# Layer-1 MLP: weight-block sums and weight splits moved from VectorE into transfers issued by GpSimd

## The chip, the cores and the metric

The kernel runs on one core of one Trainium2 chip. The metric is the device time of one execution in microseconds (us), as the median of several runs of the same program. Lines are named as in the profile (L887 is line 887 of the kernel before); the changed kernel has ten lines more ahead of most of them, so that its listings show L93, L94, L95 for the new helper and L1218 for what was L1208.

## The reference

The model is a two-layer trunk over 512 latent tokens and 256 context tokens of width 1024. Layer 0 mixes tokens with an mLSTM, layer 1 with windowed attention, and each mixer is followed by a squared-ReLU MLP of hidden width 4096. The change touches only the MLP of layer 1, which sees the latent tokens alone:

```python
def _sq_relu_mlp(u, w1, w2):
    return jnp.square(jax.nn.relu(u @ w1)) @ w2
...
h = h + mod_l[5] * _sq_relu_mlp(_modulate(_rms_norm(h, norm_ffn[i]), mod_l[3], mod_l[4]),
                                ffn_w1[i], ffn_w2[i])
...
return _rms_norm(h, final_norm)
```

All inputs are float32, and the result must keep more accuracy than one pass of TensorE in its reduced float32 type (called fp32r in the profile).

## The kernel before, in words

**Splits.** Every matrix operand is split in two fp32r parts: `hi`, the value cast to fp32r, and `lo`, the value minus `hi`. A product is then three matmuls (`mm3`, L96 to L98): hi by hi, hi by lo, lo by hi. A split (`split`, L884) is one ScalarE copy into `whi` (L887) and one VectorE subtraction into `wlo` (L888).

**Weight units and the ring.** Weights come in units of 128 partitions by 1024 float32 values (512 KB). `unit` (L73) loads a unit into a buffer named `raw` by a transfer issued on SP's queue (L80) and splits it into `whi` and `wlo`. These buffers stand in a ring with 4 `whi`, 4 `wlo` and 3 `raw` buffers. So a unit may be loaded into `raw` before a `whi` buffer comes free, and only the split waits for the buffer.

**The MLP of layer 1** (`ffn1`, with its list of weight units from `plan1`) treats the second matrix product as products of 2 by 2 blocks: tokens in two halves, hidden features in two halves, output columns in two halves. Seven block products instead of eight are enough when sums of blocks are multiplied. The work goes in four steps, `steps1`: three steps of 8 hidden tiles of 128 features and one of 4; the last 4 hidden tiles are done plainly. Each step has two parts:

- the w1 part (`hidden`): for each hidden tile one unit of `w1`, 24 matmuls of 512 columns. In the first step the first four units are taken together, in pieces of 256 columns, the later halves unit by unit.
- the w2 part (`product`): seven products, in the order 1, 2, 3, 5, 6, 7, 4 by number, each with one or two units of `w2`. The blocks of `w2` are called 11, 12, 21, 22 (feature half, output half) and lie in buffers named `wb`. `less` (L1208) forms the differences of blocks in place on VectorE: 12-11 first, then 22-12, 22-11 and 22-21 as the products ask for them. The sums of the hidden blocks are formed on VectorE in `second` (L1313 to L1315), the seven results are put together in `join`.

**The order.** Python code writes the instructions in the order of `plan`: after each unit of work that TensorE has finished, `feed` takes the next entry of the list, so that four units stand ahead of TensorE at any time. A scheduler then gives each engine its own order, which is in-order at run time: an instruction that waits holds up everything behind it on its engine, transfers that the engine issues among them. Before the change GpSimd (POOL) issues no transfer; all weights come by SP's queue.

**Buffers for transfers.** The kernel's last function makes the program with `dynamic_dma_scratch_size=512` (L1997); the change leaves that as it is.

Of the kernel before, what the change touches and what calls it, by code (L numbers as in the profile page):

```python
# [21 lines left out]
P = 128  # L22
D = 1024
KT = D // P
NL = 512
# [31 lines left out]
class Trunk:  # L57
# [15 lines left out]
    def unit(self, src, eng=None):  # L73

        nc = self.nc
        if len(src.shape) == 3:
            src = src.rearrange("m p c -> p m c")
        n = int(np.prod(src.shape[1:]))
        raw = self.ring.tile([P, D], F32, name="raw", tag="raw", bufs=self.nraw)[:, :n]
        nc.sync.dma_start(out=raw if len(src.shape) == 2 else raw.rearrange("p (m c) -> p m c", m=src.shape[1]), in_=src)  # L80
        hi = self.ring.tile([P, D], F32R, name="whi", tag="whi", bufs=self.nsplit)[:, :n]
        lo = self.ring.tile([P, D], F32R, name="wlo", tag="wlo", bufs=self.nsplit)[:, :n]
        self.split(raw, hi, lo, eng)
        if self.ada_cap and self.ada_todo and self.ada_todo[0][:2] < self.ada_cap:
            self.ada_step()
        return hi, lo

    def take(self, eng=None):
# [1101 lines left out]
    def plan1(self):  # L1190

        nc, a = self.nc, self.a
        self.steps1 = [(0, 4), (8, 4), (16, 4), (24, 2)]
        self.w2r = w2r = {}
        at = 0

        def load(b, u, n):
            def f():  # L1200
                t = w2r[b, u] = self.fp.tile([P, D], F32, name=f"wb{b}", tag=f"w{b}{u}")
                nc.sync.dma_start(out=t, in_=a["w2b"][n])
            return f

        def less(o, x, y, u):

            def f():
                nc.vector.tensor_tensor(out=w2r[o, u], in0=w2r[x, u], in1=w2r[y, u], op=ALU.subtract)  # L1208
            return f

        def w1(m, *extra):
            def f():
                r = self.unit(a["w1"][1, m])
                for x in extra:
                    x()
                return r
            return f

        def w2(b, u, *extra):
            def f():  # L1220
                hi, lo = [self.ring.tile([P, D], F32R, name=n, tag=n, bufs=self.nsplit) for n in ("whi", "wlo")]
                self.split(w2r[b, u], hi, lo)
                for x in extra:
                    x()
                return hi, lo
            return f
        self.plan, self.begun = [], []
        for base, nk in self.steps1:
            us = range(nk // 2)
            extra = []  # L1230
            for b in (12, 22, 11, 21):
                extra += [load(b, u, at + (11, 12, 21, 22).index(b) * len(us) + u) for u in us]
            extra += [less(12, 12, 11, u) for u in us]
            at += 4 * len(us)
            ms = [base + nk * i + k for k in range(nk) for i in range(2)]
            skip = 0 if base else 2
            per = -(-len(extra) // (len(ms) - skip))
            self.plan += [w1(m) for m in ms[:skip]]
            self.plan += [w1(m, *extra[per * i:per * i + per]) for i, m in enumerate(ms[skip:])]
            self.plan += [w2(b, u) for b in (11, 21) for u in us]  # L1240
            self.plan += [w2(22, u, less(22, 22, 12, u)) for u in us]
            self.plan += [w2(12, u, less(11, 22, 11, u)) for u in us]
            self.plan += [w2(22, u, less(21, 22, 21, u)) for u in us]
            self.plan += [w2(b, u) for b in (11, 21) for u in us]
# [12 lines left out]
        self.plan += [w1(m) for m in range(self.last1, 4 * KT)]  # L1257
        self.plan += [w2_plain(i) for i in range(4 * KT - self.last1)]

    def ffn1(self, u, out):  # L1260

        nc, tc, a = self.nc, self.tc, self.a
        xs = self.xs(u)
        fp = self.fp
        H = NL // 2
        tt = nc.vector.tensor_tensor
# [40 lines left out]
        def second(m, m0, k):  # L1307

            r0, r1, s34 = rt.pop(m0), rt.pop(m), rt.pop(("34", k))
            hid["12", k] = two("h12", k)  # L1310
            self.split(r1, *hid["12", k])
            s = fp.tile([P, NL], F32, name="s12", tag="s12", bufs=2)
            tt(out=s[:, 0:H], in0=r0[:, H:NL], in1=r1[:, H:NL], op=ALU.add)  # L1313
            tt(out=s[:, H:NL], in0=s[:, 0:H], in1=r0[:, 0:H], op=ALU.subtract)
            tt(out=s34[:, H:NL], in0=r1[:, 0:H], in1=s[:, H:NL], op=ALU.subtract)  # L1315
            for n, src in (("1", s), ("3", s34)):
                hid[n, k] = two("e" + n, k)
                self.split(src, *hid[n, k])
# [67 lines left out]
        def join(i):  # L1386
            a1, a3, a4, a5, a6 = [acc[p, i] for p in (1, 3, 4, 5, 6)]
            x = fp.tile([P, NL], F32, name="r", tag="r", bufs=4)
            for o, l, r, op in ((a6, a1, a6, ALU.add), (a1, kept[2, i], a1, ALU.add), (x, kept[7, i], a6, ALU.add),
                                (a6, a6, a5, ALU.add), (a3, a3, a6, ALU.add), (a4, x, a4, ALU.subtract),  # L1390
                                (a5, x, a5, ALU.add)):
                tt(out=o, in0=l, in1=r, op=op)
            for t, d, o in ((i, 0, a1), (i, 1, a3), (2 + i, 0, a4), (2 + i, 1, a5)):
                tt(out=o, in0=o, in1=self.grow[:, d * 512:(d + 1) * 512], op=ALU.mult)
                y = res[t][:, d * 512:(d + 1) * 512]
                tt(out=y, in0=y, in1=o, op=ALU.add)
        hp = []
        for n, m in enumerate(range(self.last1, 4 * KT)):
            hidden([m], square)
            hp.append(two("h12", n))  # L1400
            self.split(rt.pop(m), *hp[n])
            turn((0, 2, 1, 3)[n])
            if n % 2:
                join(n // 2)
# [600 lines left out]
```

## Time and profile before

| what | value |
|---|---|
| median of 3 runs | 1549.54 us (1549.34 to 1550.19) |
| the profiled execution | 1551.29 us, of which its span is 1549.4 us |
| MLP of layer 1 in the span | about 1208 us to the end |
| TensorE, VectorE, ScalarE, GpSimd busy | 1509.6, 1127.1, 740.2, 326.5 us |
| granted TensorE clock, mean | 0.992 |

The span runs from the first to the last instruction of the profiled execution; what is outside it is 1.9 us. PE is TensorE, DVE is VectorE, ACT is ScalarE, POOL is GpSimd, SP is the engine whose queue issues most transfers. Matmuls overlap each other, so the duration of one (389 ns) is longer than the distance between two starts.

### The profile page before, as it was taken

The numbers are of one execution on the slowest core, as the hardware profiler recorded it, in microseconds if no ns is written. First come the engines' busy times: TensorE is split into PE (matmuls) and PEld (weight loads), VectorE is DVE, ScalarE is ACT, GpSimd is POOL, SyncE is SP. The second block draws the span as 40 slices with busy tenths as digits, with TensorE's granted clock in tenths as the row PEclk, the third lists the DMA queues.
The fourth block names the chain that finished last, engine by engine and source line by source line (L and its number), as shares of the span: only waits on it lengthen the run. The fifth ranks groups of instructions, "written<-read, shape, count | busy, mean of one in ns | idle before, by whom it ended". The sixth has DMA issues, their size and how long they took to land.

```text
span 1549.4 us, 23838 instructions
## 1 busy us (share of the span) xinstructions
PE 1509.6 (97%) x9110; PEld 1355.9 (88%) x9110; DVE 1127.1 (73%) x2084; ACT 740.2 (48%) x1501; POOL 326.5 (21%) x318
## 2 busy tenths in 40 slices
PE   6999999999999999999999999999999999999998
PEld 4778888878889999999999999888887988888886
DVE  3684657488797888767676667778888875757697
ACT  4533343344573332524424355666666665545454
POOL 0322111113203222232224221243443100000000
PEclk8999999999999999999999999999999999999999
DMA  8422323234231343343443422011111424150321
GB/s 316 139 83 69 125 82 118 73 116 150 74 110 42 120 139 124 125 146 125 148 145 100 150 69 66 32 34 42 42 41 43 177 83 149 41 163 28 109 69 55
DMA packets 47848, 157.27 MB, mean 102 GB/s; under 512 B 5327, under 2 KB 8911, under 8 KB 47607
## 3 DMA queue, kind: packets, MB, share of 16 engines
q1 hardware_dynamic: 46560, 154.25, 30.3%
q8 instruction: 72, 1.18, 0.3%
q10 hardware_dynamic: 1175, 1.51, 0.3%
q14 instruction: 41, 0.34, 0.1%
HBM read 153.64 MB, written 2.10 MB: 101 GB/s over the span
## 4 chain that ended last, share of the span: by engine, by line
PE 79%; DVE 6%; issue 4%; ACT 4%; POOL 3%; DMA 1%; POOLq 0%; DVEq 0%; ACTq 0%
PE mm L96 17%; PE mm L97 16%; PE mm L98 16%; PE p L98 2%; PE p L97 2%; PE p L96 2%; PE pt L1825 2%; PE pj L96 1%; PE pj L97 1%; PE pj L98 1%; PE at L843 1%; DVE adap L262 1%; PE av L1840 1%; ACT whi L887 1%; DVE wlo L888 1%
## 5 line engine op out<-in xcount | busy, mean ns | idle before, releaser
L888 DVE TENSOR_TENSOR wlo<-raw,whi 128x1024 fp32r<-128x1024 f32 (+2 forms) x152 | 179.6, 1186 | 82.3 <-ACT whi L887 80.6
L887 ACT CAST whi<-raw 128x1024 fp32r<-128x1024 f32 (+2 forms) x155 | 154.0, 999 | 141.9 <-PE mm L97 77.4
L96 PE MATMUL mm<-uH,whi 128*128 128x512 f32 (+1 forms) x496 | 189.4, 386 | 0.0
L97 PE MATMUL mm<-uL,whi 128*128 128x512 f32 (+1 forms) x496 | 186.7, 378 | 0.7 <-DVE uL L332 0.4
L98 PE MATMUL mm<-uH,wlo 128*128 128x512 f32 (+1 forms) x496 | 186.9, 378 | 0.0
L262 DVE SCALAR_TENSOR_TENSOR adap<-raw,crow 128x1024 bf16<-128x1024 f32 x128 | 165.8, 1295 | 19.9 <-DMA raw<-ada 19.1
L96 PE MATMUL mm<-h,whi 128*128 128x384 f32 x512 | 172.9, 338 | 1.9 <-ACT h L887 1.9
L97 PE MATMUL mm<-h,whi 128*128 128x384 f32 x512 | 172.6, 337 | 0.5 <-DVE h L888 0.5
L98 PE MATMUL mm<-h,wlo 128*128 128x384 f32 x512 | 172.1, 336 | 0.0
L887 ACT CAST whi<-sum 128x512 fp32r<-128x512 f32 (+1 forms) x42 | 31.9, 761 | 165.8 <-PE mm L97 75.9
L98 PEld LDWEIGHTS mm<-uH,wlo 128*128 128x128 f32 x496 | 93.4, 188 | 17.9 <-issue 0.9
L97 PEld LDWEIGHTS mm<-uL,whi 128*128 128x128 f32 x496 | 93.6, 189 | 16.4 <-DVE uL L489 0.7
L96 PEld LDWEIGHTS mm<-uH,whi 128*128 128x128 f32 x496 | 92.9, 189 | 15.6 <-issue 0.3
L96 PEld LDWEIGHTS mm<-h,whi 128*128 128x128 f32 x512 | 96.1, 188 | 2.8 <-ACT h L887 2.8
L97 PEld LDWEIGHTS mm<-h,whi 128*128 128x128 f32 x512 | 96.1, 188 | 1.5 <-DVE h L888 1.4
L98 PEld LDWEIGHTS mm<-h,wlo 128*128 128x128 f32 x512 | 96.1, 188 | 0.0
L888 DVE TENSOR_TENSOR wlo<-wb,whi 128x1024 fp32r<-128x1024 f32 x49 | 59.2, 1221 | 35.9 <-ACT whi L887 35.8
L888 DVE TENSOR_TENSOR h<-r,h 128x384 fp32r<-128x384 f32 (+2 forms) x100 | 56.4, 568 | 34.1 <-ACT h L887 33.8
L887 ACT CAST whi<-wb 128x1024 fp32r<-128x1024 f32 x49 | 51.6, 1054 | 60.9 <-PE mm L97 27.1
L1809 POOL TENSOR_SCALAR e<-e,den 128x512 f32<-128x512 f32 (+1 forms) x64 | 49.0, 779 | 135.1 <-DVE den L1807 86.9
L98 PE MATMUL p<-t,wlo 128*128 128x384 f32 x224 | 75.4, 337 | 0.5 <-DVE wlo L888 0.5
L97 PE MATMUL p<-t,whi 128*128 128x384 f32 x224 | 75.2, 336 | 0.0
(401 smaller groups left out, 4180.0 us busy)
## 6 DMA issues: line engine op xcount, KB each, us to landing
raw<-ada SPq DMA_DIRECT2D x80, 512.0 KB, 3.6
raw<-w SPq DMA_DIRECT2D x64, 512.0 KB, 3.5
raw<-w2a SPq DMA_DIRECT2D x32, 512.0 KB, 3.5
wb<-w2b SPq DMA_DIRECT2D x28, 512.0 KB, 4.2
adaw<-ada SPq DMA_DIRECT2D x16, 512.0 KB, 7.7
hL<-xT SPq DMA_DIRECT2D x16, 256.0 KB, 3.5
raw<-wqk SPq DMA_DIRECT2D x8, 512.0 KB, 4.0
raw<-wv SPq DMA_DIRECT2D x8, 512.0 KB, 3.5
```

The costliest lines, as they stand in the source:

```text
L96: mm(out=out, lhsT=ah, rhs=bh, start=start, stop=False)
L97: mm(out=out, lhsT=ah, rhs=bl, start=False, stop=False)
L98: mm(out=out, lhsT=al, rhs=bh, start=False, stop=stop)
L262: self.tc.keep_in_program_order(nc.vector.scalar_tensor_tensor(out=pr, in0=w, scalar=0.5, in1=self.crow[:, v, :], op0=ALU.mult, op1=ALU.mu ...
L843: mm(out=o[hh][:, i * VW:(i + 1) * VW], lhsT=pw[g, d, hh][:, i, :], rhs=v[:, 3 * g + i, hh, :], start=False, stop=i == 2)
L887: keep(self.nc.scalar.copy(out=hi, in_=src))
L888: keep((eng or self.nc.vector).tensor_tensor(out=lo, in0=src, in1=hi.bitcast(F32), op=ALU.subtract))
L1809: nc.gpsimd.tensor_scalar(out=out[ii][:, :W], in0=out[ii][:, :W], scalar1=den[:, ii:ii + 1], scalar2=1.0, op0=ALU.mult, op1=ALU.mult)
L1825: nc.tensor.transpose(out=pt[:, i * P:(i + 1) * P], in_=ps_[i][:, n * P:(n + 1) * P], identity=self.ident)
L1840: mm(out=o, lhsT=vv, rhs=ph, start=n == 0, stop=False)
```

## The change

- Each unit of `w1` in layer 1 no longer passes through `raw`. `unit_dma` loads it from HBM straight into `whi` with a transfer that casts; ScalarE writes the negative of `whi` into `wlo` (`Copy` with scale -1, L94); a second transfer from HBM adds the unit onto `wlo`. Both transfers are issued by POOL (L93, L95).
- The block differences of `w2` become sums formed by transfers that add onto the block in place, issued by POOL (`more`, L1218): 12 += 11 first, then 22 += 12, and 21 += 22. The buffer of block 11 is loaded a second time, with block 12 by SP's queue, and block 22 is added onto it from HBM.
- The signs of the block products are turned to fit: in `second` and `join` some additions become subtractions and the other way round; two operations of `join` have other operands. Their number and sizes stay.

```diff
+    def unit_dma(self, src):
+        nc = self.nc
+        hi, lo = [self.ring.tile([P, D], F32R, name=n, tag=n, bufs=self.nsplit) for n in ("whi", "wlo")]
+        nc.gpsimd.dma_start(out=hi, in_=src)
+        nc.scalar.activation(out=lo, in_=hi.bitcast(F32), func=AF.Copy, scale=-1.0)
+        nc.gpsimd.dma_start(out=lo, in_=src, accum_op=ALU.add)
         return hi, lo
...
-        def less(o, x, y, u):
+        def more(o, x, u, n=None):
...
-                nc.vector.tensor_tensor(out=w2r[o, u], in0=w2r[x, u], in1=w2r[y, u], op=ALU.subtract)
+                nc.gpsimd.dma_start(out=w2r[o, u], in_=w2r[x, u] if n is None else a["w2b"][n], accum_op=ALU.add)
...
-                r = self.unit(a["w1"][1, m])
+                r = self.unit_dma(a["w1"][1, m])
...
-            for b in (12, 22, 11, 21):
-                extra += [load(b, u, at + (11, 12, 21, 22).index(b) * len(us) + u) for u in us]
-            extra += [less(12, 12, 11, u) for u in us]
+            for b in (11, 12, 21, 22):
+                extra += [load(b, u, block(b, u)) for u in us]
+            extra += [more(12, 11, u) for u in us]
...
-            self.plan += [w2(b, u) for b in (11, 21) for u in us]
-            self.plan += [w2(22, u, less(22, 22, 12, u)) for u in us]
-            self.plan += [w2(12, u, less(11, 22, 11, u)) for u in us]
-            self.plan += [w2(22, u, less(21, 22, 21, u)) for u in us]
+            self.plan += [w2(11, u, load(11, u, block(12, u)), more(11, 22, u, block(22, u))) for u in us]
+            self.plan += [w2(21, u) for u in us]
+            self.plan += [w2(22, u, more(22, 12, u)) for u in us]
+            self.plan += [w2(12, u) for u in us]
+            self.plan += [w2(22, u, more(21, 22, u)) for u in us]
             self.plan += [w2(b, u) for b in (11, 21) for u in us]
```

How the change moves instructions is read from the two programs. First POOL. Before, the last rows of its list are these: the sums of squares of the norm ahead of the MLP (`ssB`), its power (`rc`), and then nothing until the four powers of the final norm.

```order
L295 TENSOR_TENSOR nAuH_12565<-nAuH_12565,nAuL_12566 128x256
L313 TENSOR_TENSOR rc<-rs,mhalf 128x2
L295 TENSOR_TENSOR ssB<-ssB,sq 128x256 x6
L313 TENSOR_TENSOR rc<-rs,mhalf 128x2
L1425 TENSOR_TENSOR ss_15627<-ss_15627,mhalf 128x1 x4
```

In the changed program the same place begins so; `w` in a row is the layer's `w1` in HBM, `wb_13088` and `wb_13090` are the two units of block 12, `wb_13079` and `wb_13081` those of block 11.

```order
L305 TENSOR_TENSOR ssB<-ssB,sq 128x256
L93 DMA whi<-w 128x1024
L305 TENSOR_TENSOR ssB<-ssB,sq 128x256 x3
L93 DMA whi<-w 128x1024
L305 TENSOR_TENSOR ssB<-ssB,sq 128x256
L95 DMA wlo<-w 128x1024
L305 TENSOR_TENSOR ssB<-ssB,sq 128x256
L95 DMA wlo<-w 128x1024
L323 TENSOR_TENSOR rc<-rs,mhalf 128x2
L93 DMA whi<-w 128x1024 x3
L1218 DMA wb_13088<-wb_13079 128x1024
L95 DMA wlo<-w 128x1024 x3
```

Four transfers now stand among the sums and ahead of the power, and behind it the transfers of the first step follow one another, the `lo` of the fifth unit behind three `whi` transfers and one block sum.

Second, POOL at the passage from the first step's w2 part to the second step's w1 part, where before it has no row at all. With the buffers' numbers: `wb12_13782` and `wb12_13784` are block 12 of the second step, `whi_13768` and `wlo_13769` are the first unit of its `w1`.

```order
L1218 DMA wb12_13782<-wb11_13773 128x1024
L1218 DMA wb12_13784<-wb11_13775 128x1024
L93 DMA whi_13768<-w1 128x1024
L93 DMA whi_13777<-w1 128x1024
L95 DMA wlo_13769<-w1 128x1024
L93 DMA whi_13816<-w1 128x1024
L95 DMA wlo_13778<-w1 128x1024
L93 DMA whi_13825<-w1 128x1024
L95 DMA wlo_13817<-w1 128x1024
```

The first unit's cast now stands behind the two sums for block 12, and its `lo` behind the second unit's cast. Over the whole program POOL issues 92 transfers: 32 casts, 32 additions onto `wlo`, 28 additions onto blocks.

Third, VectorE at the same passage, before. The rows are the splits and differences of the last two products of the first step (`wb11`, `wb21`), the first differences of the second step, and the splits of its first units.

```order
L888 TENSOR_TENSOR wlo_13705<-wb11_13282,whi_13704 128x1024
L1208 TENSOR_TENSOR wb12_13778<-wb12_13778,wb11_13828 128x1024
L888 TENSOR_TENSOR wlo_13739<-wb21_13304,whi_13738 128x1024
L1208 TENSOR_TENSOR wb12_13780<-wb12_13780,wb11_13830 128x1024
L888 TENSOR_TENSOR wlo_13743<-wb21_13306,whi_13742 128x1024
L888 TENSOR_TENSOR wlo_13775<-raw_13772,whi_13774 128x1024
L888 TENSOR_TENSOR wlo_13785<-raw_13782,whi_13784 128x1024
L888 TENSOR_TENSOR wlo_13825<-raw_13822,whi_13824 128x1024
```

In the changed program the split of the last block is followed at once by the work on the hidden values:

```order
L898 TENSOR_TENSOR wlo_13739<-wb21_13277,whi_13738 128x1024
L1319 TENSOR_TENSOR s34_13873<-r_13859 128x256
L898 TENSOR_TENSOR h11_13870<-r_13859,h11_13869 128x256
L1327 TENSOR_TENSOR s12_13911<-r_13859,r_13900 128x256
L1328 TENSOR_TENSOR s12_13911<-s12_13911,r_13859 128x256
```

All block differences and all splits of `w1` are gone from VectorE's list there. On SP's queue 32 loads of `raw` are gone, and 7 loads of `w2` (block 12 into the buffer of block 11) are new.

More of the change, by code (lines that the diff above doesn't have):

```diff
@@ L85, in unit @@
             self.ada_step()
+        return hi, lo
+    def unit_dma(self, src):
[4 more added lines that the diff above has]
+        nc.gpsimd.dma_start(out=lo, in_=src, accum_op=ALU.add)
         return hi, lo
@@ L1230, in plan1, with block @@
             extra = []
-            for b in (12, 22, 11, 21):
-                extra += [load(b, u, at + (11, 12, 21, 22).index(b) * len(us) + u) for u in us]
-            extra += [less(12, 12, 11, u) for u in us]
+            def block(b, u, at=at, n=len(us)):
+                return at + (11, 12, 21, 22).index(b) * n + u
+            for b in (11, 12, 21, 22):
+                extra += [load(b, u, block(b, u)) for u in us]
+            extra += [more(12, 11, u) for u in us]
             at += 4 * len(us)
@@ L1312, in second @@
             s = fp.tile([P, NL], F32, name="s12", tag="s12", bufs=2)
-            tt(out=s[:, 0:H], in0=r0[:, H:NL], in1=r1[:, H:NL], op=ALU.add)
+            tt(out=s[:, 0:H], in0=r0[:, H:NL], in1=r1[:, H:NL], op=ALU.subtract)
             tt(out=s[:, H:NL], in0=s[:, 0:H], in1=r0[:, 0:H], op=ALU.subtract)
-            tt(out=s34[:, H:NL], in0=r1[:, 0:H], in1=s[:, H:NL], op=ALU.subtract)
+            tt(out=s34[:, H:NL], in0=r1[:, 0:H], in1=s[:, H:NL], op=ALU.add)
             for n, src in (("1", s), ("3", s34)):
@@ L1389, in join @@
             for o, l, r, op in ((a6, a1, a6, ALU.add), (a1, kept[2, i], a1, ALU.add), (x, kept[7, i], a6, ALU.add),
-                                (a6, a6, a5, ALU.add), (a3, a3, a6, ALU.add), (a4, x, a4, ALU.subtract),
-                                (a5, x, a5, ALU.add)):
+                                (a3, a3, a5, ALU.add), (a3, a3, a6, ALU.subtract), (a4, x, a4, ALU.add),
+                                (a5, a5, x, ALU.subtract)):
                 tt(out=o, in0=l, in1=r, op=op)
```

## The prediction

> **What bounds the kernel now.** I read the page's head first, then the busy time by stretches, then the groups of instructions in the MLP of layer 1, and last single rows at the places where the changed lists differ. The head of the page, its slices of POOL, and its DMA queues:
>
> ```profile
> span 1549.4 us, 23838 instructions
> PE 1509.6 (97%) x9110; PEld 1355.9 (88%) x9110; DVE 1127.1 (73%) x2084; ACT 740.2 (48%) x1501; POOL 326.5 (21%) x318
> ...
> POOL 0322111113203222232224221243443100000000
> ...
> q1 hardware_dynamic: 46560, 154.25, 30.3%
> q10 hardware_dynamic: 1175, 1.51, 0.3%
> ```
>
> TensorE is the bound, POOL is idle in the last eight slices (the MLP that is changed), and the two queues that moved data are hardware queues, of SP and ACT; POOL issued nothing. The stretches below are the w1 and w2 parts of the first steps, then the rest (PE, PEld, DVE, ACT, POOL busy, clock, DMA share, GB/s):
>
> ```profile
> 1215.00:1250.00 35.00, 35.00 (x216) 31.55 (x215) 28.50 (x50) 25.03 (x49) 0.00 (x0) 1.00 0.49 188
> 1250.00:1290.00 40.00, 40.00 (x178) 33.14 (x177) 27.89 (x28) 22.42 (x28) 0.00 (x0) 1.00 0.40 128
> 1290.00:1335.00 45.00, 45.00 (x201) 37.24 (x200) 23.54 (x36) 25.62 (x39) 0.00 (x0) 1.00 0.23 74
> 1335.00:1372.00 37.00, 37.00 (x165) 30.65 (x164) 32.76 (x37) 16.38 (x18) 0.00 (x0) 1.00 0.44 141
> ...
> 1454.00:1490.00 36.00, 36.00 (x164) 29.60 (x162) 27.34 (x39) 18.99 (x28) 0.00 (x0) 1.00 0.11 34
> 1490.00:1549.00 59.00, 52.53 (x247) 43.24 (x245) 47.68 (x75) 25.63 (x47) 2.18 (x4) 0.97 0.22 78
> ```
>
> PE is busy for the whole of every stretch from 1215 to 1490 us, at the full clock, while DVE is not. So nothing taken from DVE there can shorten the span; PE already waits for nobody. Only the two ends could gain.
>
> **What goes.** The groups between 1205 and 1500 us (busy, mean of one, idle before):
>
> ```profile
> L888 DVE TENSOR_TENSOR wlo<-raw,whi 128x1024 fp32r<-128x1024 f32 x30 | 36.7, 1224 | 35.4 <-ACT whi L887 35.0
> L1208 DVE TENSOR_TENSOR wb<-wb,wb 128x1024 f32<-128x1024 f32 x28 | 33.6, 1220 | 2.4 <-DMA wb<-w2b 2.3
> L887 ACT CAST whi<-raw 128x1024 fp32r<-128x1024 f32 x29 | 30.5, 1053 | 44.9 <-PE mm L97 21.4 <-PE mm L98 10.8 <-PE kept L98 10.7
> ```
>
> DVE loses 28 differences of 1.22 us and 32 subtractions of 1.22 us, some 73 us in all, hidden under PE; worth nothing. ACT's 32 copies of 1.05 us become 32 scaled copies of the same size: nothing. The turned signs change neither number nor size: nothing. At the start one subtraction lies on the chain that ended last (start, length):
>
> ```profile
> 1189.75 1.15 DVE wlo L888
> ...
> 1202.49 0.75 POOL ssB L295
> ...
> 1208.32 0.72 POOL rc L313
> ```
>
> Its 1.15 us are the gain that I count.
>
> **What a unit of w1 costs now, and what covers it.** Before, `raw` was loaded ahead, and from a free `whi` buffer to a ready unit it took 1.05 (ACT) and 1.22 (DVE), 2.3 us. Now the load itself waits for the buffer: POOL issues, the cast lands, ACT copies, POOL issues again, the addition lands. The trace has no transfer of POOL's; the nearest rows are loads of the same 512 KB by SP (issue in ns, landing in us, min/median/max) and a small POOL operation:
>
> ```profile
> L80 SPq DMA_DIRECT2D raw<-w x32: 327/328/328, 1156.5 to 1488.5; - x32
> ...
> DMA to landing us min/median/max: 3.4/3.6/8.7
> L295 POOL TENSOR_TENSOR ssB<-ssB,sq x6: 732/738/802, 1200.9 to 1206.2; 128x256 f32<-128x256 f32 x6
> L1809 POOL TENSOR_SCALAR e<-e,den 128x640 f32<-128x640 f32 x21 | 18.6, 898 | 37.2 <-DVE den L1807 26.5 <-DVE nb L1793 4.0 <-ACT ph L1830 3.9
> ```
>
> Issue: between 0.33 us (SP's) and 0.90 us (a POOL instruction over 640 columns); I take 0.75, since it is POOL's work. The cast moves what a load moves: 3.6 us. The addition reads two streams of 512 KB where a load reads one. What one stream costs the 16 engines comes from the window 1150:1549:
>
> ```profile
> q1 hardware_dynamic: 9936, 35.13, 26.6%
> ```
>
> 35.13 MB in 26.6% of 399 us, 106 us, is 331 GB/s, 1.6 us for 512 KB (in the burst shown below 1.3 us). So the addition lands after 3.6 us at the least (the second stream free) and 7.2 us at the most (two loads in turn); I take 5.0, one stream more, because the start and the end of a transfer need not be paid twice. The unit's path is then 0.75+3.6+1.05+0.75+5.0 = 11.15 us (8.9 with both lower ends, 13.65 with both upper ends).
>
> The Trainium skill, "DMA: Bandwidth & Descriptors", section "Latency and other measured facts", puts the first byte of a transfer that GpSimd issues at about 1 us against 0.6 us for SP's; by 1.0 us an issue the path would be 11.65 us and the sum below some 4 us more. No run here shows it yet.
>
> The cover at a passage between steps, from the trace (ACT rows, then PE rows; a buffer comes free where the cast's wait ends):
>
> ```profile
> 1275.32 1.22 DVE L888 TENSOR_TENSOR wlo<-wb,whi 128x1024 fp32r<-128x1024 f32 x1 [0.62 <-ACT whi L887]
> ...
> 1283.26 1.05 ACT L887 CAST whi<-raw 128x1024 fp32r<-128x1024 f32 x1 [2.54 <-PE kept L98]
> ...
> 1289.87 0.39 PE L96 MATMUL mm<-uH,whi 128*128 128x512 f32 x1
> 1290.09 0.39 PE L97 MATMUL mm<-uL,whi 128*128 128x512 f32 x1
> 1290.32 0.39 PE L98 MATMUL mm<-uH,wlo 128*128 128x512 f32 x1
> ```
>
> From 1283.26 to the first matmul at 1289.87 are 6.6 us, one product. The cover in the first step, where four units end close together:
>
> ```profile
> 1225.76 1.05 ACT L887 CAST whi<-raw 128x1024 fp32r<-128x1024 f32 x1 [0.96 <-PE mm L97]
> ...
> 1230.00 0.40 PE L96 MATMUL mm<-uH,whi 128*128 128x512 f32 x1
> ```
>
> 4.2 us. Elsewhere in a w1 part a buffer comes free three units ahead of its next use; a unit is 24 matmuls 0.227 us apart (1289.87, 1290.09, 1290.32), 5.4 us, so 16.3 us cover 11.15: no cost, unless the path grows by 5 us.
>
> **The sum.**
> - Start: POOL's row of four transfers among the norm's sums holds the chain `ssB`, `rc` up by four issues of 0.75, 3.0 us; less the 1.15 of DVE: +2.
> - First step, fifth unit: 11.15 - 4.2 = 7.0. Two casts and a block sum stand ahead of its `lo` on POOL; their issues fit into the first landing, their transfers hold it up by about one stream, 1.6: +9 with rounding.
> - Passages to the second and third step: 11.15 - 6.6 = 4.6. Ahead of the cast stand two block sums (12 += 11). They wait for the reload of block 11, whose buffer is last read at 1276.5 (1275.32 plus 1.22); it lands at 1280.1 and the second at about 1281.5, so the sums' transfers, 3 us each, fill the engines until about 1287, and the cast issued at 1284 loses 3 us. The second unit's cast stands ahead of the `lo`: 1.4. Together +9 each, 18.
> - Passage to the last step, with one sum and half the blocks: +5.
> - The four plain units at the end, fed one at a time: +2, a guess of one issue and one stream.
> - w2 parts: additions on blocks are asked for a product or more ahead (22 += 12 is issued behind the split for product 3, read by product 6 with product 5 between); 5.75 us stand against 5.4 us a product and two products of lead: no cost. Seven more loads on SP (1.6 us each) and 32 fewer: no cost.
>
> 2+9+18+5+2 = 36, so the profiled span goes from 1549.4 to about 1585, and with 1.9 around it to 1587. That profiled execution was 1.75 us above the median (1551.29 against 1549.54); against the median the sum gives 1586, and I say 1587. With the ends of the path, 8.9 and 13.65, the passages cost 4 to 12 each and the first step 5 to 14: 17 to 53, 1566 to 1603; that is this case's own range.
>
> What the transfers already do to each other is seen when SP's queue issues eleven at once (window 1215:1250):
>
> ```profile
> GB/s 412 393 84 0 0 0 0 0 0 75 239 398 360 346 393 412 398 403 426 417 412 421 412 426 365 80 23 5 0 9 0 47 201 342 28 0 0 0 0 0
> ...
> wb<-w2b SPq DMA_DIRECT2D x7, 512.0 KB, 6.9
> raw<-w SPq DMA_DIRECT2D x4, 512.0 KB, 8.0
> ```
>
> In such a burst a load lands after 7 to 8 us instead of 3.6. A full step now holds 10 loads, 8 casts and 16 additions: 18 at 1.6 and 16 at 3.2 us are 80 us of the engines in a step of 82 us (1290 to 1372), at the burst's rate 65. There is little air for anything slower.
>
> **Rivals.**
> - *POOL's transfers become the bound.* If an addition must be over before the next is issued, POOL needs 5.75 us for each of 16 and 0.75 for each of 8 casts, 98 us in a step of 82: 16 us more in each of three steps, with the passages 36+3x16 = 84, about 1634; if an addition takes the engines 4.8 us instead of 3.2, the same. With casts in turn too (8 of 4.35), 36+3x45 = 171. For it: PE needs all of a step already, and DMA has 2 us left by the slower rate. Against it: SP's queue shows eleven transfers in flight. Chance 0.30. The Trainium skill ("DMA: Bandwidth & Descriptors", "The descriptor swizzle", and "SBUF — State Buffer", on its size) says that GpSimd's descriptors, 16 bytes each and 9 on the read side for 128 partitions, lie in the scratch that this kernel cuts to 512 bytes: by my estimate 32 on a ring, three plain transfers, or one addition if it needs 17. No run here shows it yet.
> - *The transfers are quick*: landing at the lower ends and never in each other's way, only the first step and three passages cost, 4.7+3x2.3 = 12, less 1.15 at the start: 1553 to 1565. Chance 0.13.
> - *Faster.* If cast and addition each landed within 2.3 us of their wish to be issued (6.6 - 1.05 = 5.5 for both, with two issues of 0.33), the passages would be covered and the 1.15 us at the start, with a second split taken off DVE there, would remain: 1547. The point that decides is the unit's path against 6.6 us; the quickest landing of 512 KB is 3.4. Chance 0.05 for faster, 0.05 for no difference.
> - *POOL holds up attention*: the first cast stands between two of the attention's scalings and waits for a buffer of the ring. It would add 1 to 5 us to any case; not one of its own.
>
> **How the numbers follow.** The forecast's case has 0.47, the bound on POOL 0.30, quick transfers 0.13, faster 0.05, no difference 0.05. A measurement of this kernel tells about 0.2% (3 us) from no change. Slower is 0.47+0.30+0.13 = 0.90. The range leaves out faster and no difference (0.10) a little of the quick case (0.02) and the upper part of the bound on POOL (0.08): from 1557 to 1660.
>
> **What would show it.** In the changed profile: PE's idle time sits before L106 and L108, ended by DMA, at four places (fifth unit, three passages), 5 to 10 us each, and is near zero in w2 parts; POOL rows L93, L95, L1218 show the issue; the landing of L95 and L1218 is 4 to 7 us; DVE is some 73 us less busy with nothing gained. If PE also waits within w1 or w2 parts, the bound on POOL is right; if L93 lands under 2.3 us I am wrong on the sign.

## The result, and the profile after

The changed kernel takes 1660.73 us (1657.24 to 1666.17, four runs) against 1549.87 us before: a ratio of 1.0713 (1.0679 to 1.0747). It is 111 us slower, on the side that was forecast and just outside the range.

The head of the page, its slices of PE and of the clock, and the queue that is new:

```profile
span 1658.6 us, 23956 instructions
PE 1539.0 (93%) x9110; PEld 1369.1 (83%) x9110; DVE 1063.9 (64%) x2024; ACT 739.6 (45%) x1501; POOL 397.5 (24%) x410
...
PE   7999999999999999999999999999976879599798
...
PEclk9999999999999999999999999999997979899899
...
q0 software_dynamic: 13248, 48.24, 14.2%
```

DVE is 63 us less busy and nothing is gained by it. The span is 109.2 us longer, and two subtractions split that. PE's idle time (span less busy) went from 39.8 to 119.6 us, +79.8. PE's busy time went from 1509.6 to 1539.0 us, +29.4, for the same 9110 matmuls, so some of them take longer. Nearly all of both lies in the last eleven slices; of the others only the first reads otherwise (7 for 6, clock 9 for 8).

Where PE waits, in the window 1190:1658 (us in total, times, longest):

```profile
PE mm L106 <- DMA whi<-w: 39.0, 9, 11.9
PE mm L108 <- DMA wlo<-w: 36.2, 13, 8.1
```

What POOL waits for in the same window; "issue" is time in which it waited for nothing that the profile shows:

```profile
POOL wb L1218 <- issue: 73.0, 14, 6.2
POOL wlo L95 <- issue: 48.6, 12, 5.0
...
POOL whi L93 <- PE mm L108: 29.4, 8, 16.2
...
POOL whi L93 <- issue: 21.1, 11, 4.4
```

143 us of POOL's time have no visible cause. Its rows in order of time (start, length, idle before) show a pattern:

```profile
1243.91 0.91 POOL L95 DMA_DIRECT2D wlo<-w  x1 [3.98 <-ACT e L897]
1249.68 0.87 POOL L95 DMA_DIRECT2D wlo<-w  x1 [4.86 <-issue]
1255.51 0.89 POOL L95 DMA_DIRECT2D wlo<-w  x1 [4.96 <-issue]
1261.47 0.88 POOL L1218 DMA_DIRECT2D wb<-wb  x1 [5.07 <-issue]
1262.02 0.89 POOL L93 DMA_DIRECT2D whi<-w  x1
```

Additions start 5.8 to 6.0 us apart, about the time that one needs to land (L95: 5.3/5.5/6.8 us, min/median/max), while a cast follows an addition at once. The issue of a transfer costs POOL 0.89 us for an addition and 0.55 us for most casts.

### The profile page after: what moved, and what is told of

Same layout as the page of the kernel before. It is cut to its first block, busy times and chain, and to the rows that moved or that the text cites. A ratio compares the mean times of both kernels' runs of the same rounds, so it can differ in the third digit from the quotient of the medians.

```text
span 1658.6 us, 23956 instructions
## 1 busy us (share of the span) xinstructions
PE 1539.0 (93%) x9110; PEld 1369.1 (83%) x9110; DVE 1063.9 (64%) x2024; ACT 739.6 (45%) x1501; POOL 397.5 (24%) x410
## 3 DMA queue, kind: packets, MB, share of 16 engines
q0 software_dynamic: 13248, 48.24, 14.2%
## 4 chain that ended last, share of the span: by engine, by line
PE 57%; issue 15%; DMA 8%; DVE 7%; ACT 5%; POOL 5%; POOLq 0%; SPq 0%; ACTq 0%; DVEq 0%
PE mm L108 11%; PE mm L106 11%; PE mm L107 11%; DMA wb<-w2b 2%; PE p L107 2%; PE p L108 2%; PE p L106 2%; DMA whi<-w 2%; PE pt L1839 2%; ACT whi L897 1%; DMA wb<-wb 1%; DMA wlo<-w 1%; DVE adap L272 1%; PE pj L106 1%; PE pj L107 1%
## 5 line engine op out<-in xcount | busy, mean ns | idle before, releaser
L106 PE MATMUL mm<-uH,whi 128*128 128x512 f32 (+1 forms) x496 | 199.3, 406 | 39.7 <-DMA whi<-w 39.0
L108 PE MATMUL mm<-uH,wlo 128*128 128x512 f32 (+1 forms) x496 | 195.4, 397 | 36.3 <-DMA wlo<-w 36.2
L107 PE MATMUL mm<-uL,whi 128*128 128x512 f32 (+1 forms) x496 | 194.6, 394 | 1.5 <-DVE uL L342 1.2
L898 DVE TENSOR_TENSOR wlo<-raw,whi 128x1024 fp32r<-128x1024 f32 (+1 forms) x120 | 141.3, 1182 | 54.4 <-ACT whi L897 54.2
L106 PE MATMUL mm<-h,whi 128*128 128x384 f32 x512 | 172.9, 338 | 1.7 <-ACT h L897 1.7
L108 PE MATMUL mm<-h,wlo 128*128 128x384 f32 x512 | 172.1, 336 | 0.0
L897 ACT CAST whi<-raw 128x1024 fp32r<-128x1024 f32 (+2 forms) x123 | 120.3, 984 | 91.1 <-PE mm L107 49.5
L108 PEld LDWEIGHTS mm<-uH,wlo 128*128 128x128 f32 x496 | 97.4, 197 | 62.1 <-DMA wlo<-w 42.9
L106 PEld LDWEIGHTS mm<-uH,whi 128*128 128x128 f32 x496 | 98.1, 199 | 61.2 <-DMA whi<-w 37.1
L107 PEld LDWEIGHTS mm<-uL,whi 128*128 128x128 f32 x496 | 98.5, 199 | 18.7 <-DVE uL L342 1.4
L106 PEld LDWEIGHTS mm<-h,whi 128*128 128x128 f32 x512 | 96.1, 188 | 2.6 <-ACT h L897 2.6
L94 ACT ACTIVATE wlo<-whi 128x1024 fp32r<-128x1024 f32 x32 | 33.9, 1059 | 141.5 <-DMA whi<-w 137.4
L108 PEld LDWEIGHTS mm<-h,wlo 128*128 128x128 f32 x512 | 96.1, 188 | 0.0
L108 PE MATMUL p<-t,wlo 128*128 128x384 f32 x224 | 75.4, 337 | 0.4 <-DVE wlo L898 0.4
```

The costliest lines, as they stand in the source:

```text
L94: nc.scalar.activation(out=lo, in_=hi.bitcast(F32), func=AF.Copy, scale=-1.0)
L106: mm(out=out, lhsT=ah, rhs=bh, start=start, stop=False)
L107: mm(out=out, lhsT=ah, rhs=bl, start=False, stop=False)
L108: mm(out=out, lhsT=al, rhs=bh, start=False, stop=stop)
L897: keep(self.nc.scalar.copy(out=hi, in_=src))
L898: keep((eng or self.nc.vector).tensor_tensor(out=lo, in0=src, in1=hi.bitcast(F32), op=ALU.subtract))
```

## The experiments

The sum of the prediction knows one kind of loss, PE's idle time. So for every kernel the table gives two differences to the profile of before: span less PE's busy time (idle), against 39.8 us, and PE's busy time, against 1509.6 us. Both are read from one execution of each kernel, and executions of the kernel before alone range from 1548.5 to 1559.8 us, so a few us between two rows tell nothing. Ratios are to runs of before on the same chip.

| kernel | us | ratio (95% interval) | idle | busy |
|---|---|---|---|---|
| changed | 1660.7 | 1.0713 (1.0679 to 1.0747) | +79.8 | +29.4 |
| scratch 448 | 1664.6 | 1.0720 (1.0677 to 1.0762) | +79.8 | +29.0 |
| scratch 576 | 1608.4 | 1.0358 (1.0318 to 1.0399) | +36.4 | +20.5 |
| scratch 1024 | 1601.9 | one run | +30.8 | +19.9 |
| scratch 1792 | 1606.8 | 1.0352 (1.0324 to 1.0379) | +32.9 | +24.0 |
| sums only, 512 | 1553.1 | 1.0010 (0.9993 to 1.0028) | -0.6 | +2.5 |
| units only, 512 | 1608.5 | 1.0368 (1.0342 to 1.0395) | +32.9 | +23.8 |
| units only, 1792 | 1589.2 | 1.0234 (1.0203 to 1.0265) | +20.6 | +14.8 |
| spare pair, 1792 | 1600.2 | 1.0300 (1.0276 to 1.0325) | +30.2 | +20.9 |
| units and spare pair, 1792 | 1578.4 | 1.0172 (1.0143 to 1.0201) | +17.2 | +12.0 |
| plain copies, 1792 | 1579.7 | 1.0195 (1.0160 to 1.0231) | +16.2 | +12.0 |
| cast only, 512 | 1563.1 | 1.0081 (1.0055 to 1.0107) | +4.4 | +6.7 |
| PE filled, 1792 | 1615.2 | 1.0394 (1.0369 to 1.0419) | +30.1 | +33.6 |
| subtraction repeated | 1556.8 | 1.0022 (1.0004 to 1.0040) | +3.1 | +3.9 |
| hops of SP | 1592.2 | 1.0270 (1.0238 to 1.0302) | +31.2 | +15.7 |

**The scratch for descriptors.** The theory: an addition fills more than half of the places in the scratch of 512 bytes, so POOL waits until one has landed before it can issue the next.

```diff
-    nc = bacc.Bacc("TRN2", target_bir_lowering=False, num_devices=1, dynamic_dma_scratch_size=512)
+    nc = bacc.Bacc("TRN2", target_bir_lowering=False, num_devices=1, dynamic_dma_scratch_size=1792)
```

> The changed kernel with its scratch for POOL's transfers raised from 512 to 1792 bytes a partition, nothing else. Theory R (the scratch holds one addition at a time: an addition waits on POOL until the one before has landed, 5.8 us apart in the changed profile): POOL's waits that nothing explains (143 us in the MLP) go below 20 us, additions follow each other 0.9 us apart, and only the passages and the fifth unit cost, 26 us plus what a lower granted clock adds: 1575 to 1600 us. Rival E (an addition keeps the 16 engines busy for some 5 us, so transfers are the bound whatever the scratch): the waits move from POOL to the landings, the landing of an addition grows from 5.5 to over 10 us, and the time stays at 1645 to 1665 us.

> The same with 1024 bytes. Theory R: if a descriptor takes 16 bytes and an addition 17 places, three additions fit (51 of 64), and hardly more are ever in flight: within 8 us of the kernel with 1792 bytes. Rival E: 1645 to 1665 us as with 512.

1606.8 and 1601.9 us: 54 us of the 111 were the scratch, and with 1792 bytes POOL's waits without a visible cause are 1.6 us where they were 143. But 57 us stayed, so that the time is above theory R's 1575 to 1600 us and far below its rival's; the table says what they are: 33 us of idle time and 24 us of longer matmuls.

Whether the scratch works by a step or by degrees was then tried with the smallest change on either side:

> The changed kernel with the descriptor scratch at 576 bytes instead of 512: 36 places of 16 bytes instead of 32. Theory R17 (an addition takes 17 places and a cast 9, so two additions, 34, fit for the first time): additions follow each other without POOL's unexplained waits of 5 us, and nearly all of the 54 us between 512 and 1792 bytes is won by these 64 bytes: 1602 to 1618. Rival G (more scratch helps by degrees, or the second addition needs another count): 64 bytes of the 512 that lead to 1024 win about an eighth of the way, 1648 to 1660.

> The changed kernel with the descriptor scratch at 448 bytes, 28 places. Theory R17: still one addition, or one addition and a cast (26), or three casts (27), as with 32 places: the same time as 512 bytes, 1654 to 1668. Rival G (by degrees): 8 to 25 us slower than 512 bytes, 1669 to 1686.

1608.4 and 1664.6 us. It is a step: 64 bytes more win 52 us, all that 1792 bytes win, and 64 bytes less cost nothing. POOL's waits in the kernel with 448 bytes and its rows with 576 bytes:

```profile
POOL wb L1218 <- issue: 67.2, 13, 6.3
POOL wlo L95 <- issue: 49.8, 12, 5.1
```

```profile
1243.53 0.89 POOL L95 DMA_DIRECT2D wlo<-w  x1 [1.74 <-ACT r L1306]
1245.90 0.89 POOL L95 DMA_DIRECT2D wlo<-w  x1 [1.47 <-ACT h L897]
1249.79 0.87 POOL L95 DMA_DIRECT2D wlo<-w  x1 [3.00 <-issue]
1252.24 0.86 POOL L1218 DMA_DIRECT2D wb<-wb  x1 [1.58 <-issue]
```

With 576 bytes a second addition goes 2.4 us behind the first, and the third waits; with 448 they go singly. That two additions need more than 512 and at most 576 bytes is shown by the step and these rows; how many places one takes is not. The Trainium skill, "DMA: Bandwidth & Descriptors", counts 9 read descriptors on each DMA engine for a transfer of 1 MiB to 128 partitions ("The descriptor swizzle") and 16 bytes for one ("Terms"). The trace agrees with the 9: POOL's queue moved 13248 packets in 92 transfers, 144 each, 9 on each of 16 engines. The estimate that the prediction drew from the page, 17 places for an addition, puts two at 544 bytes; the step between 512 and 576 agrees with it, as it would with 18. The packets do not show the 17: their number is the same with plain copies.

**Which half of the change.** Each part alone, with the scratch of the changed kernel:

```diff
-                r = self.unit_dma(a["w1"][1, m])
+                r = self.unit(a["w1"][1, m])
```

> The changed kernel with w1 loaded and split as before (raw, ACT, DVE); only the block sums of w2 are made by adding transfers (scratch 512). Theory R: the sums are asked for a product or more ahead and 28 additions one at a time fill 28 x 5.8 = 162 us of 300: no more than 5 us from the kernel before, 1547 to 1555. Rival E: the other half of the loss, 1590 to 1615.

> The kernel before, with only the units of layer 1's w1 loaded by cast, copy and addition (scratch 512); block differences of w2 stay on VectorE. Theory R: casts and additions alternate and hold each other up less, the passages have no block sums ahead of them: 25 to 55 us slower than before, 1575 to 1605. Rival E: 32 of 60 additions remain, so about half of the loss, 55 us: 1600 to 1615.

The first kernel has the block sums by transfers and `w1` as before; the second has only the `w1` units changed. 1553.1 us is no change that can be told from before, and far from rival E's 1590 to 1615. 1608.5 us is half of the loss; it lies in E's range and just above theory R's 1575 to 1605, so it is the sums and the larger scratch that speak against E, not the units. The sums by themselves wait on POOL as in the changed kernel, and PE does not notice:

```profile
POOL wb L1218 <- DMA wb<-w2b: 110.1, 7, 23.5
...
POOL wb L1218 <- issue: 54.1, 8, 12.1
```

```profile
1300.00:1350.00 50.00, 50.00 (x222) 41.39 (x221) 31.64 (x48) 30.88 (x45) 3.96 (x5) 1.00 0.50 130
1350.00:1400.00 50.00, 49.16 (x216) 40.16 (x215) 28.00 (x37) 22.55 (x30) 3.52 (x4) 1.00 0.71 207
```

The columns are those of the stretches in the prediction: clock 1.00 with the DMA engines 71% busy. The sums cost something only beside the units: 1660.7 against 1608.5 with 512 bytes.

**The idle time that the larger scratch leaves.** Three kernels with 1792 bytes: the block sums back on DVE; a spare pair of buffers (two of the idle `raw` buffers) for the first unit of each step; and both.

```diff
+        if spare:
+            hi, lo = [self.ring.tile([P, D], F32R, name="raw", tag="raw", bufs=self.nraw) for _ in range(2)]
+        else:
             hi, lo = [self.ring.tile([P, D], F32R, name=n, tag=n, bufs=self.nsplit) for n in ("whi", "wlo")]
...
-                r = self.unit_dma(a["w1"][1, m])
+                r = self.unit_dma(a["w1"][1, m], m in (0, 8, 16, 24))
```

> Only the w1 units by cast, copy and addition, the block sums on DVE as before, and a descriptor scratch of 1792 bytes. Theory S (in the changed kernel with the larger scratch the block sums stand ahead of the casts on POOL and on the DMA engines at the passages between steps, and that is part of the remaining loss): PE waits fall from 34 us to 19 to 25, its busy time is 10 to 18 us above before, time 1576 to 1592. Rival P (only the unit's own path of about 11 us against its cover costs): PE waits stay at 30 to 36 us, time 1601 to 1610. The descriptor ring's part in the units alone is the distance to 1608.5 with 512 bytes.

> The changed kernel with the scratch of 1792 bytes, and the first unit of each step takes its pair of buffers from the raw loads' ring, which nothing else uses in this MLP; its cast need not wait for a buffer of the whi ring. Theory P (the wait at a passage is the unit's path less its cover): three passages lose 8, 8 and 5 us of waits, most of which goes, and with it 4 to 6 us of lowered clock: 1582 to 1593. Rival S (the cast is held on POOL behind the block sums and by full DMA engines, whatever its buffer): within 5 us of 1606.8, 1600 to 1611.

> Block sums on DVE, scratch of 1792 bytes, and the first w1 unit of each step in a spare pair of buffers. With the sums away the waits were 21 us, with the spare pair alone 31. Theory PS (both hold the same passages up, so that the one is worth little without the other): waits 5 to 14 us, ratio 1.008 to 1.018. Rival (they are the same gain; what is left is the unit's own path): waits 17 to 22 us, ratio 1.020 to 1.026.

Without the sums the ratio is 1.0234, 12 us of idle time less: as theory S. With the spare pair alone it is 1.0300: the 1600.2 us are at the lower end of rival S's range (1600 to 1611) and outside theory P's. Both together give 1.0172, in theory PS's range for the time, with 17 us of waits above its 5 to 14. Its reason, that the one is worth little without the other, is not borne out: from 1.0352 the sums' absence takes 0.012 and the spare pair 0.005 alone, and both together 0.018, about their sum. PE's waits in the kernel with the scratch of 1792 bytes, and with the spare pair:

```profile
PE mm L108 <- DMA wlo<-w: 21.0, 7, 4.9
PE mm L106 <- DMA whi<-w: 12.8, 6, 3.7
```

```profile
PE mm L111 <- DMA wlo<-w: 30.8, 8, 7.9
...
PE mm L109 <- DMA whi<-w: 0.3, 1, 0.3
```

The spare pair does what it should: nobody waits for `whi` any more. But the wait moved on to `wlo`, 21.0 to 30.8 us. Why, POOL's and ACT's rows show at the passage to the second step of the kernel with 1792 bytes, where the window 1308:1316 has the DMA engines 100 to 104% busy by the trace's count:

```profile
1306.46 0.87 POOL L1218 DMA_DIRECT2D wb<-wb  x1 [14.28 <-DVE wlo L898]
1307.78 0.86 POOL L1218 DMA_DIRECT2D wb<-wb  x1 [0.45 <-issue]
1308.34 0.88 POOL L93 DMA_DIRECT2D whi<-w  x1
1309.42 0.55 POOL L93 DMA_DIRECT2D whi<-w  x1 [0.21 <-issue]
1319.56 0.88 POOL L95 DMA_DIRECT2D wlo<-w  x1 [9.59 <-ACT wlo L94]
```

```profile
1318.14 1.06 ACT L94 ACTIVATE wlo<-whi 128x1024 fp32r<-128x1024 f32 x1 [13.07 <-DMA whi<-w]
```

```profile
1308.00:1312.00 4.00, 4.00 (x20) 3.30 (x19) 0.00 (x0) 0.00 (x0) 1.77 (x3) 1.00 1.00 222
1312.00:1316.00 4.00, 2.38 (x11) 1.64 (x9) 0.00 (x0) 0.00 (x0) 0.00 (x0) 1.00 1.04 230
```

Two block sums stand ahead of the first cast on POOL, which had waited 14.3 us for the buffers that DVE was to free. All four transfers then start within 3 us and share full engines, and ACT can copy only 9.8 us after the first cast was issued, where the shortest landing of a cast is 3.7 us. The kernel with the spare pair shows the same at this place: two sums, two casts, and the copy 9.9 us after the first cast.

**The accumulating transfer.** The changed kernel with 1792 bytes and every accumulating transfer a plain copy; and the kernel before with only `whi` by a casting transfer, beside SP's load of `raw`:

```diff
+    def unit_cast(self, src):
+        nc = self.nc
+        raw = self.ring.tile([P, D], F32, name="raw", tag="raw", bufs=self.nraw)
+        nc.sync.dma_start(out=raw, in_=src)
+        hi, lo = [self.ring.tile([P, D], F32R, name=n, tag=n, bufs=self.nsplit) for n in ("whi", "wlo")]
+        nc.gpsimd.dma_start(out=hi, in_=src)
+        nc.vector.tensor_tensor(out=lo, in0=raw, in1=hi.bitcast(F32), op=ALU.subtract)
+        return hi, lo
```

> The changed kernel with the scratch of 1792 bytes, in which every accumulating transfer is a plain copy of the same bytes (the additions themselves are left out). Theory D (the second stream that an addition reads makes it land after 5.5 us instead of 3.7 and fills the engines at the passages): PE waits fall from 34 to 8 to 18 us, PE busy 6 to 14 us above before, ratio 1.009 to 1.021. Rival F (the chain of two transfers and a copy costs by its length, whatever the second reads): PE waits within 6 us of 34, ratio 1.030 to 1.038.

> The kernel before, scratch of 512 bytes; of the w1 units only whi comes by a casting transfer of POOL's, beside SP's load of raw, and DVE forms wlo = raw - whi as before; block sums on DVE. Theory A (it is the accumulating transfer behind the copy that makes the unit's path longer than its cover; with the cast alone it is 0.55 + 3.7 + 1.22 = 5.5 us against 6.6): PE waits for DMA at most 8 us in the MLP, ratio to before 1.000 to 1.007. Rival K (that a weight's transfer waits for a free buffer at all, or its place on POOL, costs as much): PE waits 15 to 30 us and longer matmuls, ratio 1.015 to 1.03.

1.0195 and 17.8 us of waits: theory D. As a copy the `wlo` transfer is issued in 0.53 us instead of 0.89 and lands after 4.2 us instead of 5.7 (medians, both with 1792 bytes). From the two pages (the queue's packets, MB and share of the 16 DMA engines' span; median landing), first with additions, then with copies:

```profile
q0 software_dynamic: 13248, 48.24, 14.2%
...
wlo<-w POOLq DMA_DIRECT2D x32, 512.0 KB, 5.7
```

```profile
q0 software_dynamic: 13248, 48.24, 9.3%
...
wlo<-w POOLq DMA_DIRECT2D x32, 512.0 KB, 4.2
```

For the same bytes by the page's count, the copies take less of the engines' time. Adding instead of copying is worth 1.5 us of landing and half of the idle time; how much of that is the second stream and how much the issue was not told apart. The cast alone costs 1.0081, just above theory A's 1.007 and far from K: of its 4.8 us of waits for weights, 3.5 are one wait at the fifth unit, where the prediction had put the thinnest cover. An extra cast of 32 units is nearly free; what is dear is the addition behind it.

**The longer matmuls.** What follows a pause, in rows of PE at the passage to the second step with 1792 bytes:

```profile
1325.09 0.79 PE L108 MATMUL mm<-uH,wlo 128*128 128x512 f32 x1 [4.59 <-DMA wlo<-w]
1325.68 0.63 PE L106 MATMUL mm<-uH,whi 128*128 128x512 f32 x1
1326.11 0.63 PE L107 MATMUL mm<-uL,whi 128*128 128x512 f32 x1
...
1329.09 0.63 PE L108 MATMUL mm<-uH,wlo 128*128 128x512 f32 x1
1329.52 0.43 PE L106 MATMUL mm<-uH,whi 128*128 128x512 f32 x1
1329.79 0.39 PE L107 MATMUL mm<-uL,whi 128*128 128x512 f32 x1
1330.02 0.39 PE L108 MATMUL mm<-uH,wlo 128*128 128x512 f32 x1
```

For 4.4 us starts are 0.43 us apart instead of 0.23, and the granted clock is 0.50; then all is as before:

```profile
1324.00:1328.00 4.00, 2.91 (x7) 2.33 (x8) 0.00 (x0) 1.06 (x1) 0.00 (x0) 0.50 1.02 230
...
1332.00:1336.00 4.00, 4.00 (x20) 3.30 (x19) 0.85 (x2) 1.64 (x3) 1.45 (x2) 1.00 0.73 178
```

Is it the pause that does this, or the transfers of POOL's queue? Three kernels were to tell. In the first, DVE repeats its subtraction for the first unit of three steps; in the second, PE runs more matmuls ahead of the passages of the kernel with 1792 bytes; in the third, the finished `wlo` of six units is copied seven times by SP's queue, with POOL idle.

```diff
+        for _ in range(again):
+            nc.vector.tensor_tensor(out=lo, in0=raw, in1=hi.bitcast(F32), op=ALU.subtract)
```

```diff
+                for _ in range({8: 24, 16: 24, 24: 16}.get(m[at[0]], 0)):
+                    nc.tensor.matmul(out=pss[0], lhsT=self.identr, rhs=xs[g](0)[0], start=True, stop=True)
```

```diff
+            for _ in range(hops):
+                nc.sync.dma_start(out=b.bitcast(F32), in_=a.bitcast(F32))
+                a, b = b, a
```

> The kernel before, with the subtraction that makes wlo repeated on DVE for the first unit of the second, third and last step (5, 8 and 11 more times, the same values again); nothing goes through POOL's queue. A unit then takes 1.05 + 1.22 x (1 + n) us against a cover of 6.6 us: PE should pause about 2, 5 and 9 us, 11 to 16 us in all. Theory C (a pause of PE of about 3 us or more is followed by some 4 us at half the granted clock, which costs about 2 us of longer matmuls each): PE's busy time 3 to 7 us above that of before, time 1564 to 1573. Rival T (it is the transfers of POOL's queue that lower the clock): PE's busy time within 1 us of before, clock 0.99 around the pauses, time 1560 to 1566.

> The changed kernel with the scratch of 1792 bytes, and ahead of the first product of w1 in the second, third and last step PE runs 24, 24 and 16 more matmuls of 512 columns (5.4, 5.4 and 3.6 us) whose sum the first real matmul overwrites: work in place of a pause. Theory C (the pause lowers the clock): no matmul behind those passages at half clock or only few, time 4 to 9 us under 1606.8: 1597 to 1603. Rival T (the clock falls with the transfers): the matmuls behind the passages stay at about 0.43 us apart, time 1604 to 1611.

> The kernel before, with nothing on POOL's queue; for the first two w1 units of the second, third and last step the finished wlo is copied seven times between two buffers by SP's hardware queue before PE may use it. Three pauses of PE of some 8 to 14 us, 25 to 40 us in all. Theory C (the pause lowers the clock): matmuls behind each pause 0.43 us apart for about 4 us, PE busy 4 to 10 us above before in all. Rival T (POOL's transfers lower it): matmuls 0.23 us apart from the first, PE busy within 2 us of before.

The first missed its aim: the repeats were spread among DVE's other work and PE's order had other matmuls ahead of them, so that PE paused at none of the three passages (idle +3.1 us). It tells nothing on the clock. The second missed its time, 1.0394 where theory C had 0.2 to 0.6% under 1.0352. Its 64 extra matmuls (14.5 us) took the place of the wait for `whi` only: pauses for `wlo` of 4.1, 3.6 and 1.7 us stayed at the three passages, the first two again followed by half clock, further waits came up later in the steps, and the idle time is 30.1 us against 32.9. Less the 14.5 us, PE's busy time is +19.1 against +24.0. That fits the theory without deciding it. The third decides. No transfer goes through POOL, three pauses are there, and behind the first:

```profile
1319.26 0.79 PE L106 MATMUL mm<-uH,wlo 128*128 128x512 f32 x1 [10.63 <-DMA wlo<-raw]
1319.85 0.63 PE L104 MATMUL mm<-uH,whi 128*128 128x512 f32 x1
...
1323.27 0.50 PE L106 MATMUL mm<-uH,wlo 128*128 128x512 f32 x1
1323.60 0.39 PE L104 MATMUL mm<-uH,whi 128*128 128x512 f32 x1
```

```profile
1312.00:1316.00 4.00, 0.00 (x0) 0.00 (x0) 0.00 (x0) 1.04 (x1) 0.00 (x0) 0.66 1.01 350
1316.00:1320.00 4.00, 0.74 (x2) 0.64 (x3) 1.22 (x1) 0.00 (x0) 0.00 (x0) 0.50 0.80 237
1320.00:1324.00 4.00, 4.00 (x12) 3.15 (x11) 0.00 (x0) 0.00 (x0) 0.00 (x0) 0.56 0.82 323
```

The clock falls during the pause, and 4.3 us at half speed follow it, without POOL's queue. PE's busy time is 15.7 us above before, more than the expected 4 to 10; the three pauses account for about 7 of it (nine matmuls 0.2 us longer and a slow first one behind each). About 2 more lie at the start of the MLP, behind a pause of 1.95 us that the kernel before has too: 24 matmuls of 256 columns are 0.21 us apart there instead of 0.12. The rest was not traced. So the pause is enough; and with the sums alone, 28 transfers of POOL's and no long pause, the clock stays at 1.00. Nor is it full DMA engines by themselves: in the window 1308:1312 of the kernel with 1792 bytes, shown above, they are 100% busy at clock 1.00.

The Trainium skill, "TensorE: Matmul & The Clock Gate", part 1 and "HAM oscillation", says that PE's clock is halved after an idle window of about 3.4 us and given back after as long a busy one, with windows that run freely. The traces agree in part: half clock lasts 4.3 and 4.4 us behind the pauses above, and 5 to 13 matmuls of 512 columns, some 3 to 6 us, over all kernels here. But shorter pauses bring it too: from 1190 us on every pause of 2.8 us or more was followed by it, most of those between 2.0 and 2.8 us, and the one of 1.95 us at the start of the MLP in some executions and not in others.

## Why the prediction was wrong

**The waits of the forecast's case were right, place by place, for a kernel that was not the changed one.** The prediction's 36 us hold for additions in flight together, and that is the kernel with 1792 bytes: idle +32.9. By place, from PE's rows there: the start 2.4 more than before (predicted 2), the fifth unit and its neighbours 3.7+1.1+3.6 = 8.4 (9), the two passages 3.7+0.5+4.6 = 8.8 and 3.3+4.7 = 8.0 (9 each), the last passage 4.9 (5), the tail 1.6 (2); 34 in all. The unit's path, by the shortest landings of the changed kernel's profile, is 0.55+3.7+1.06+0.89+5.3 = 11.5 us against 11.15; the cast's issue was lower than taken (0.55 for 0.75), the addition's higher (0.89). The Trainium skill, "DMA: Bandwidth & Descriptors", "Latency and other measured facts", has about 1 us to the first byte of such a transfer; the path of 11.65 us worked out from it is near the 11.5 by luck: the issues in the changed kernel took 0.55 and 0.89 us, not 1, and the landing of the addition 5.3 where 5.0 was taken.

**First step that failed: the choice between the cases.** "The sum" and "w2 parts: no cost" let additions overlap, because SP's queue showed eleven transfers in flight. That was another queue. The rival "POOL's transfers become the bound" had the mechanism, an addition over before the next is issued, and its waits in sum: 84 us against the measured 79.8. By place they differ: for a full step it had 9 us at the passage and 16 within the parts, and the changed kernel shows 16 at the passage (11.8+1.5+3.1 for the second step) and 4 within. The estimate beside it, one addition in 512 bytes, was right as well, and 512 was in the kernel's text. It was held at 0.30 because no row showed it; but the row held against it did not bear on it either.

**Second step that failed: a term that is missing in every case.** The sum added waits to a fixed amount of PE work. A pause is also followed by some 3 to 6 us at half clock and by a slow first matmul. PE's busy time is +29.4 us in the changed kernel and +24.0 with 1792 bytes; by the lengths of the matmuls in PE's rows, some 23 and 14 us of these are matmuls at half clock, and the rest was not told apart. In the table the added busy time is 0.36 to 0.74 of the added idle time wherever that is over 10 us (the filled kernel less its 14.5 us). With it the rival would have said about 1634 + 29 = 1663 and the forecast 1587 + 24 = 1611; the times are 1660.7 and 1606.8. The range's upper end, 1660, rested on a rival that counted waits alone (about 1634).

**What was right.** The sign; the time taken from DVE (63 us by the page, where 73 was worked out; the difference was not traced) worth nothing; landings of additions 4.5 to 6.8 us against 4 to 7; waits before L106 and L108 ended by DMA. The sign that would mark the rival, PE waiting within the w1 and w2 parts, is there too, in the middle of the second step's w1 part:

```profile
1371.62 0.50 PE L108 MATMUL mm<-uH,wlo 128*128 128x512 f32 x1 [2.26 <-DMA wlo<-w]
```

POOL did not hold up attention: until 1190 us PE's busy time in stretches of 200 us agrees with before within 0.5 us. "Two sums ahead of the cast" was named as 3 us of a passage; the kernels without sums show 12 us of idle time for it over all. With 1792 bytes and no sums the passages to the second and third step are 4.4 and 4.7 us, as the path less its cover, 4.6, had it.

No version here beats the kernel before; the nearest that still moves work, the block sums alone, cannot be told from it (1.0010).

## What to carry to other kernels

Before work is handed to transfers that GpSimd issues, look at how much room the program gives their descriptors: here 64 bytes decide whether additions go singly or in pairs, worth 52 us. Price a pause of TensorE at the pause plus 1.5 to 3 us for the slow matmuls behind it: here every pause of 2.8 us or more had them, and most of 2.0 to 2.8 us (5 to 13 matmuls 0.2 us longer, and a slow first one). A load that used to run ahead into its own buffer loses its cover when it is made to write the final buffer in two dependent transfers; count the whole path from the free buffer, not the time of a transfer.

## What the runs showed of the hardware that was not expected

- An accumulating transfer of 512 KB is issued in 0.89 us and lands after 5.5 us (median), a casting one is mostly issued in 0.55 us and lands after 3.7 us at the quickest; as a plain copy the first is issued in 0.53 us and lands after 4.2 us (median).
- The scratch for descriptors acts as a step: 448 and 512 bytes give 1664.6 and 1660.7 us, 576, 1024 and 1792 bytes 1608.4, 1601.9 and 1606.8 us.
- POOL's wait for room in it carries no releaser in the trace: it reads as "issue", 143 us in the changed kernel, up to 6.2 us at a time.
